# Shared-bank sums of recombined products and a second bank set for the down projections

## The chip, the cores and the metric

The kernel runs on one core of a Trainium2 chip. The metric is the device time of one execution in microseconds (us), the median of the runs. Names of engines: PE is TensorE (matmuls), PEld its weight loads, DVE is VectorE, ACT is ScalarE, POOL is GpSimd, SP the engine whose queue issues the DMAs. A bank is one 128 x 512 fp32 buffer of PSUM, where matmuls leave their sums.

## The reference

A backbone of two layers over 512 latent tokens and 256 context tokens, 1024 wide, in fp32. Each layer has a mixer and a feed-forward part with a convolution; the change is inside the latter alone.

```python
D_MODEL = 1024; SEQ = 512; CTX_LEN = 256; DEPTH = 2; D_FF = 2816; CONV_W = 3
...
def conv_ffn(h, w_up, conv_w, conv_b, w_down):
    t_len = h.shape[1]
    up = h @ w_up
    gate, val = up[..., :D_FF], up[..., D_FF:]
    pad = CONV_W // 2
    gp = jnp.pad(gate, ((0, 0), (pad, pad), (0, 0)))
    gate_c = conv_b
    for j in range(CONV_W):
        gate_c = gate_c + gp[:, j:j + t_len] * conv_w[j]
    return (jax.nn.silu(gate_c) * val) @ w_down
...
    for l in range(DEPTH):
        with_ctx = l < DEPTH - 1
...
        xl = xl + g2 * conv_ffn(modulate(xl, norm_ffn_w[l], sh2, sc2), ffn_w_up[l],
                                ffn_conv_w[l], ffn_conv_b[l], ffn_w_down[l])
        if with_ctx:
            xc = xc + cg2 * conv_ffn(modulate(xc, norm_ffn_w[l], csh2, csc2), ffn_w_up[l],
                                     ffn_conv_w[l], ffn_conv_b[l], ffn_w_down[l])
```

Layer 0 carries latent and context tokens (768 columns), layer 1 the latent tokens alone (512 columns).

## The kernel before

Activations are held transposed: 128 features on the partitions, tokens as columns. Every fp32 operand is kept as a high and a low part, and `mm3` (lines 501 to 503) makes one product of three matmuls: high x high, high x low, low x high. The weights come by DMA as raw fp32 and are split on the way: ACT casts the high part (L390, L490), and POOL or DVE subtracts it to get the low part (L392, L492).

The feed-forward part goes over 22 tiles of 128 features (D_FF = 2816). The first two tiles of each layer are computed plainly. Tiles 2 to 21 use seven half-sized products, j = 0 to 6, in place of eight: the tokens are halved into `nh` columns (384 in layer 0, 256 in layer 1), the input halves are combined once, the weight halves are summed per tile by DVE (`sum`, L381 to L383 and L387), and each product is 4 x 3 = 12 matmuls. `up_products` adds the products up to the gate (`gate`, two halves `g1`, `g2`) and the value (`u`, `w`). Before the change each product has a bank of its own in turn, and DVE does one copy (L1178) and seven adds (L1172) per tile.

What follows per tile is here called the tail: ACT's first convolution step (L1198), four DVE steps (L1200, L1202), Silu on ACT (L1204), the multiply by `u` on POOL (L1205) and by `w` on DVE (L1206), the cast to the high part on ACT (L1208) and the low part on POOL (L1209).

After a group of tiles comes its down projection (`out_pass`): 8 output blocks `m`, for each of which the matmuls over the group's tiles go into a bank per token segment, and DVE adds the gated result to the residual stream `xl`, `xc` (`residual`, L1016). In layer 0 the groups are 3, 3, 3, 3, 3, 3 and 4 tiles, and a group's down projection runs in one piece after the first tile of the next group. In layer 1 the groups are 2 and then 4 at a time, and two blocks of the down projection run after each tile, 24 matmuls of 512 columns.

There are eight banks, four with the tag `mm` and four with `aux`; a bank is handed out again when its last reader is done. `u` and `w` come from the pool `tp` under the tag `t2k`, 3 buffers, which some of the weight sums share. Each engine works through its own queue in order. A scheduler sets the order in the queues from the order of the code, dependences and priorities (`tc.high_priority`); `_Stream` decides when the next weights are loaded and split, by the units in `PROD_UNITS`; `PROD_ON_V` lists the products whose low part DVE makes, per layer; `PROD_OWN` those with a buffer outside the common pool.

Of the kernel before, what the change touches and what calls it, by code (L numbers as in the profile page):

```python
# [11 lines left out]
F32 = mybir.dt.float32  # L12
# [4 lines left out]
ALU = mybir.AluOpType  # L17
# [3 lines left out]
P = 128  # L21
# [13 lines left out]

FF_GROUPS = ((3, 3, 3, 3, 3, 3, 4), (2, 4, 4, 4, 4, 4))
FF_PLAIN = (2, 2)
PROD_ON_V = ((2,), (0, 1, 2, 3))
PROD_OWN = ((6,), (0, 4, 5, 6))
PROD_UNITS = ((0,), (1, 2, 3), (4,), (5,), (6,))  # L40
PROD_USE = (0, 1, 2, 3, 4, 5, 6)
PROD_FIRST = (0, 1, 2, 3, 4, 5, 6)

# [1 line left out]
def _ff_per(layer, g):  # L47

    return 8 // FF_GROUPS[layer][g]


def prod_order(layer, t):

    return PROD_FIRST if t == FF_PLAIN[layer] else PROD_USE


def _ff_order(layer):
# [234 lines left out]
class _Stream:  # L292
# [4 lines left out]
    def __init__(self, nc, w, raw_pool, hl_pool, order, offs, split, last_pool, sums):  # L297
        self.nc, self.w, self.order, self.offs = nc, w, order, offs
        self.raw_pool, self.hl_pool, self.split, self.last_pool, self.sums = raw_pool, hl_pool, split, last_pool, sums
        self.raw, self.hl = {}, {}  # L300
        self.n_dma = self.n_unit = self.pos = 0
        self.units, self.items = [], []
        i = 0
        while i < len(order):
            kind, t = order[i]
            if kind[:2] == "up" and FF_PLAIN[int(kind[2:])] <= t < NFF:
                for u in PROD_UNITS:
                    self.units.append((i, u))
                self.items += [(kind, t, j) for j in prod_order(int(kind[2:]), t)]
                i += 2  # L310
            else:
                self.units.append((i, None))
                self.items.append(order[i])
                i += 1
        self.live, self.own = {}, set()
        self.part = None
# [104 lines left out]
def backbone(ctx: ExitStack, tc, w, xt, ada, vec, cst, msk, rop, wst, bs, pew, out):  # L421
    nc = tc.nc
    V, S, G, T = nc.vector, nc.scalar, nc.gpsimd, nc.tensor
# [72 lines left out]
    ws = _Stream(nc, w, wraw, whl, chunk_order(), chunk_offsets(), split, lambda l, dt=F32R: last_pool[l](dt),  # L496
                 lambda l, n: sum_pool[l](n))

    def mm3(ps, a, b, first, last):

        T.matmul(ps, a[0], b[0], start=first, stop=False)  # L501
        T.matmul(ps, a[0], b[1], start=False, stop=False)  # L502
        T.matmul(ps, a[1], b[0], start=False, stop=last)  # L503


    bg = {"gla": deque(), "ada": deque(), "sum": deque()}
# [508 lines left out]
    def residual(xs, ps, gate):  # L1015
        V.scalar_tensor_tensor(xs, ps, gate, xs, op0=ALU.mult, op1=ALU.add)  # L1016

    def out_pass(key, nk, src, dst, gcol, each, chunks=None):

        per = 8 // nk  # L1020
        for m in range(KD):
            if chunks is not None and m // per not in chunks:
                continue
            if m % per == 0:
                wh, wl = ws.next((key, m // per))
            d = dst(m)
            ps = [bank("mm") for _ in d]
            for k in range(nk):
                o = (m % per * nk + k) * P
                a = (wh[:, o:o + P], wl[:, o:o + P])  # L1030
                for s in range(len(d)):
                    mm3(ps[s][:, 0:d[s].shape[-1]], a, src[s][k], k == 0, k == nk - 1)
                if k % 3 == 2:
                    tick()
            for s in range(len(d)):
                residual(d[s], ps[s][:, 0:d[s].shape[-1]], gcol(m, s))
            each(m)
# [14 lines left out]
    def ffn(layer, X, src, parts, late, down_last):  # L1052
# [106 lines left out]
        def up_products(t, gate):  # L1159

            ts = [[(tv(i, kk)[:, 0, :], tv(i, kk)[:, 1, :]) for kk in range(4)] for i in range(3)]
            rhs = [xq(0, n1), ts[1], xq(4, n2), ts[0], ts[2], xq(4, n1), xq(0, n2)]

            def product(j, ps):
                h, l = ws.next((f"up{layer}", t, j))
                for kk in range(4):
                    mm3(ps[:, 0:nh], (h[:, kk * P:(kk + 1) * P], l[:, kk * P:(kk + 1) * P]), rhs[j][kk],
                        kk == 0, kk == 3)
                return ps[:, 0:nh]

            def add(o, a, b):
                V.tensor_tensor(o, a, b, op=ALU.add)  # L1172

            b1, b2, b4, b3 = bank("mm"), bank("mm"), bank("aux"), bank("aux")
            u = tp.tile([P, nh], F32, tag="t2k", name="u")
            w_ = tp.tile([P, nh], F32, tag="t2k", name="w")
            g1, g2, u, w_ = gate[:, n1], gate[:, n2], u[:], w_[:]
            todo = [((0,), lambda p: V.tensor_copy(g1, p[0])), ((0, 1), lambda p: add(u, g1, p[1])),  # L1178
                    ((1, 3), lambda p: add(w_, u, p[3])), ((2, 3), lambda p: add(g2, w_, p[2])),
                    ((3, 4), lambda p: add(u, u, p[4])), ((3, 4), lambda p: add(w_, w_, p[4])),  # L1180
                    ((1, 5), lambda p: add(g1, g1, p[5])), ((3, 4, 6), lambda p: add(u, u, p[6]))]
            banks = (b1, b2, b4, b3, b1, b2, b3)
            done = {}
            for j in prod_order(layer, t):
                done[j] = product(j, banks[j])
                for need, f in [x for x in todo if all(k in done for k in x[0])]:
                    f(done)
                todo = [x for x in todo if not all(k in done for k in x[0])]
            return u, w_

        plain = FF_PLAIN[layer]
        for kind, i, *cs in seq:
            if kind == "up" and i >= plain:
                gate = t1tile()
                u, w_ = up_products(i, gate)
                t1 = t1tile()
                cw = lambda j: vcol("convw", (layer * 3 + j) * NFF + i)
                S.activation(t1[:, 0:nw], gate[:, 0:nw], AF.Identity, bias=vcol("convb", layer * NFF + i), scale=cw(1))  # L1198
                for c0, b, bc, n in merged:
                    V.scalar_tensor_tensor(t1[:, c0 + 1:c0 + n], gate[:, c0:c0 + n - 1], cw(0), t1[:, c0 + 1:c0 + n],  # L1200
                                           op0=ALU.mult, op1=ALU.add)
                    V.scalar_tensor_tensor(t1[:, c0:c0 + n - 1], gate[:, c0 + 1:c0 + n], cw(2), t1[:, c0:c0 + n - 1],  # L1202
                                           op0=ALU.mult, op1=ALU.add)
                S.activation(t1[:, 0:nw], t1[:, 0:nw], AF.Silu)  # L1204
                G.tensor_tensor(t1[:, n1], t1[:, n1], u, op=ALU.mult)  # L1205
                V.tensor_tensor(t1[:, n2], t1[:, n2], w_, op=ALU.mult)  # L1206
                a = acttile()
                S.copy(a[:, 0, 0:nw], t1[:, 0:nw])  # L1208
                G.tensor_tensor(a[:, 1, 0:nw], t1[:, 0:nw], a[:, 0, 0:nw].bitcast(F32), op=ALU.subtract)  # L1209
                acts[i] = a  # L1210
            elif kind == "up":
                psg, psv = up(i, i == 0)
                t1 = t1tile()
                cw = lambda j: vcol("convw", (layer * 3 + j) * NFF + i)
                for c0, b, bc, n in merged:
                    S.activation(t1[:, c0:c0 + n], psg[b][:, 0:n], AF.Identity, bias=vcol("convb", layer * NFF + i),
                                 scale=cw(1))
                    V.scalar_tensor_tensor(t1[:, c0 + 1:c0 + n], psg[b][:, 0:n - 1], cw(0), t1[:, c0 + 1:c0 + n],
                                           op0=ALU.mult, op1=ALU.add)
                    V.scalar_tensor_tensor(t1[:, c0:c0 + n - 1], psg[b][:, 1:n], cw(2), t1[:, c0:c0 + n - 1],  # L1220
                                           op0=ALU.mult, op1=ALU.add)
                S.activation(t1[:, 0:nw], t1[:, 0:nw], AF.Silu)
                for c0, b, bc, n in merged:
                    V.tensor_tensor(t1[:, c0:c0 + n], psv[b][:, 0:n], t1[:, c0:c0 + n], op=ALU.mult)
                a = acttile()
                S.copy(a[:, 0, 0:nw], t1[:, 0:nw])
                G.tensor_tensor(a[:, 1, 0:nw], t1[:, 0:nw], a[:, 0, 0:nw].bitcast(F32), op=ALU.subtract)
                acts[i] = a
                if i == plain - 1:
                    drain("sum")  # L1230
                    replace()
            else:
                n = groups[i]
                tl = [acts[starts[i] + j] for j in range(n)]
                pairs = [[(a[:, 0, c0:c0 + w_], a[:, 1, c0:c0 + w_]) for a in tl] for c0, b, bc, w_ in merged]
                if i == len(groups) - 1:
                    down_last(f"down{layer}_{i}", n, pairs)
                else:
                    out_pass(f"down{layer}_{i}", n, pairs, xdst, lambda m, s: mods[layer][:, 40 + m, s:s + 1],
                             lambda m: None, cs[0])  # L1240


    xl, xc = load_x()
# [189 lines left out]
    A = []  # L1433
# [389 lines left out]
```

## Time and profile before

| what | value |
|---|---|
| median of 3 runs | 1714.34 us (1713.84 to 1714.83) |
| the profiled execution | 1713.79 us, its span 1712.0 us |
| PE busy | 94% of the span, 11206 matmuls |
| DVE, ACT, POOL busy | 68%, 40%, 43% |
| layer 0's feed-forward stretch 540 to 965 us | PE busy 412.66 of 425.00 us |
| layer 1's feed-forward stretch 1450 to 1660 us | PE busy 194.04 of 210.00 us |

In a profile line, times are us unless marked ns. A timeline line reads: start, duration, engine, source line, operation, output<-inputs, shape, and in brackets the idle time of that engine before it and what ended it. A line of groups reads: line, engine, operation, names, shapes, count | busy, mean ns of one | idle time before, and what ended most of it. A line of stretches reads: from:to, length, then PE, PEld, DVE, ACT and POOL busy (instructions), PE's granted clock, DMA share and GB/s. Line numbers are those of the kernel that ran; the changed kernel's are 6 lower up to `out_pass`, and up to 7 higher behind `up_products`.

### The profile page before, as it was taken

How to read it: one execution, taken by the hardware profiler on the slowest of the kernel's cores; microseconds unless marked ns; L12 is line 12 of the kernel's file. 1: busy time of each engine (PE TensorE's matmuls, PEld its weight loads, DVE VectorE, ACT ScalarE, POOL GpSimd, SP SyncE). 2: the span in 40 equal slices, each digit the busy share in tenths (PEclk: the TensorE clock that was granted, in tenths of full speed). 3: DMA queues.
4: the chain of work that ended last, by engine and by line, in shares of the span. 5: the costliest groups of instructions: out<-in, count | busy, mean ns of one | idle time of the engine just before them, and what ended most of it. 6: DMA issues, size and time to landing. Idle time of an engine off the chain costs nothing.

```text
span 1712.0 us, 28429 instructions
## 1 busy us (share of the span) xinstructions
PE 1616.2 (94%) x11206; PEld 1430.8 (84%) x11206; DVE 1164.5 (68%) x2124; ACT 685.9 (40%) x1374; POOL 735.6 (43%) x456
## 2 busy tenths in 40 slices
PE   7999999989999999999999999988899989999999
PEld 6777777778899989889898888566799978888887
DVE  6347676752756756666665784777866898888884
ACT  4323333523453323233232453556554544343431
POOL 1221223344535556566564423411127356555551
PEclk9999999999999999999999999999999999999999
DMA  8453334323412122121221223632015222222222
GB/s 341 136 196 113 136 112 148 114 96 110 124 35 78 53 67 79 58 78 37 76 82 54 88 87 105 243 118 100 24 50 174 86 74 88 90 96 88 98 79 82
DMA packets 53206, 175.11 MB, mean 102 GB/s; under 512 B 5713, under 2 KB 7761, under 8 KB 53073
## 3 DMA queue, kind: packets, MB, share of 16 engines
q1 hardware_dynamic: 51632, 170.66, 30.4%
q10 hardware_dynamic: 1440, 2.64, 0.4%
q8 instruction: 88, 1.44, 0.3%
q14 instruction: 46, 0.37, 0.1%
HBM read 171.18 MB, written 2.10 MB: 101 GB/s over the span
## 4 chain that ended last, share of the span: by engine, by line
PE 62%; DVE 22%; issue 5%; POOL 4%; ACT 4%; DMA 3%; DVEq 0%; ACTq 0%; SPq 0%; POOLq 0%
PE mm L501 14%; PE mm L502 14%; PE mm L503 14%; PE aux L501 3%; PE aux L502 3%; PE aux L503 3%; DVE wp L392 3%; DMA raw<-in_w_dram 2%; PE aux L570 2%; POOL wl L492 2%; DVE qk L858 1%; DVE kt L382 1%; DVE qk L856 1%; DVE kt L383 1%; ACT wp L390 1%
## 5 line engine op out<-in xcount | busy, mean ns | idle before, releaser
L492 POOL TENSOR_TENSOR wl<-raw,wh 128x1024 fp32r<-128x1024 f32 (+6 forms) x143 | 311.3, 2179 | 508.2 <-ACT wh L490 471.0
L490 ACT CAST wh<-raw 128x1024 fp32r<-128x1024 f32 (+5 forms) x155 | 146.5, 945 | 138.2 <-PE mm L502 71.6
L392 POOL TENSOR_TENSOR wp<-sum,wp 128x512 fp32r<-128x512 f32 x80 | 111.7, 1403 | 155.8 <-ACT wp L390 155.8
L501 PE MATMUL mm<-slot,wh 128*128 128x512 f32 (+1 forms) x480 | 163.5, 341 | 13.3 <-DVE xl L1016 10.7
L502 PE MATMUL mm<-slot,wh 128*128 128x512 f32 (+1 forms) x480 | 162.3, 338 | 1.0 <-POOL slot L1209 0.7
L503 PE MATMUL mm<-slot,wl 128*128 128x512 f32 (+1 forms) x480 | 161.5, 337 | 0.0
L1016 DVE SCALAR_TENSOR_TENSOR xl<-mm,mods,xl 128x512 f32<-128x512 f32 (+1 forms) x128 | 90.8, 712 | 96.0 <-PE mm L503 95.9
L392 POOL TENSOR_TENSOR wp<-raw,wp 128x512 fp32r<-128x512 f32 x80 | 113.7, 1428 | 69.2 <-ACT wp L390 69.2
L501 PE MATMUL mm<-xt,wh 128*128 128x256 f32 (+1 forms) x384 | 135.6, 355 | 0.0
L390 ACT CAST wp<-sum 128x512 fp32r<-128x512 f32 x100 | 60.8, 620 | 186.1 <-DVE sum L387 80.3
L503 PE MATMUL mm<-xt,wl 128*128 128x512 f32 (+1 forms) x384 | 130.2, 340 | 0.0
L502 PE MATMUL mm<-xt,wh 128*128 128x512 f32 (+1 forms) x384 | 130.2, 340 | 0.0
L501 PEld LDWEIGHTS mm<-slot,wh 128*128 128x128 f32 x480 | 90.5, 189 | 27.1 <-DVE xl L1016 11.9
L501 PE MATMUL mm<-lt,wh 128*128 128x512 f32 (+2 forms) x308 | 106.9, 347 | 0.0
L503 PE MATMUL mm<-lt,wl 128*128 128x512 f32 (+2 forms) x308 | 106.4, 346 | 0.0
L502 PE MATMUL mm<-lt,wh 128*128 128x512 f32 (+2 forms) x308 | 106.3, 345 | 0.0
L390 ACT CAST wp<-raw 128x512 fp32r<-128x512 f32 x100 | 61.8, 618 | 96.3 <-PE mm L502 36.6
L502 PEld LDWEIGHTS mm<-slot,wh 128*128 128x128 f32 x480 | 90.6, 189 | 11.7 <-POOL slot L1209 1.1
L503 PEld LDWEIGHTS mm<-slot,wl 128*128 128x128 f32 x480 | 90.7, 189 | 10.4
L501 PEld LDWEIGHTS mm<-xt,wh 128*128 128x128 f32 x384 | 72.9, 190 | 25.9 <-issue 16.8
L1205 POOL TENSOR_TENSOR t<-t,u 128x384 f32<-128x384 f32 (+1 forms) x40 | 46.0, 1151 | 99.3 <-ACT t L1204 96.1
L501 PE MATMUL aux<-kt,wp 128*128 128x256 f32 x240 | 69.8, 291 | 19.7 <-DVE w L1172 19.7
(363 smaller groups left out, 4962.5 us busy)
## 6 DMA issues: line engine op xcount, KB each, us to landing
raw<-in_w_dram SPq DMA_DIRECT2D x162, 512.0 KB, 3.6
ada_t<-in_ada_dram SPq DMA_DIRECT2D x80, 512.0 KB, 4.5
raw<-in_w_dram SPq DMA_DIRECT2D x31, 384.0 KB, 3.1
wp<-in_w_dram SPq DMA_DIRECT2D x20, 512.0 KB, 4.6
kt<-in_ada_dram SPq DMA_DIRECT2D x16, 512.0 KB, 6.1
raw<-in_w_dram SPq DMA_DIRECT2D x10, 256.0 KB, 2.6
xl<-in_xt_dram SPq DMA_DIRECT2D x2, 1024.0 KB, 9.4
out_dram<-xl SPq DMA_DIRECT2D x8, 256.0 KB, 2.0
```

The costliest lines, as they stand in the source:

```text
L382: V.tensor_tensor(s2, s1, a11, op=ALU.subtract)
L383: V.tensor_tensor(s4, a12, s2, op=ALU.subtract)
L390: S.copy(h, a)
L392: e.tensor_tensor(l, a, h.bitcast(F32), op=ALU.subtract)
L490: S.copy(h, raw)
L492: e.tensor_tensor(l, raw, h.bitcast(F32), op=ALU.subtract)
L501: T.matmul(ps, a[0], b[0], start=first, stop=False)
L502: T.matmul(ps, a[0], b[1], start=False, stop=False)
L503: T.matmul(ps, a[1], b[0], start=False, stop=last)
L570: T.matmul(ps[32 * q:32 * q + 32, :], sc_pad[:, k, :], t[:, j * 512:(j + 1) * 512], start=(k == 0), stop=(k == KD - 1))
L1016: V.scalar_tensor_tensor(xs, ps, gate, xs, op0=ALU.mult, op1=ALU.add)
L1205: G.tensor_tensor(t1[:, n1], t1[:, n1], u, op=ALU.mult)
```

## The change

Products that enter the same sums are now accumulated by PE in one bank, without a new start: 0, 1 and 3 in bank A, 4 and 6 in C, 5 in B, 2 in E. Between them ACT copies the sum so far out of the bank (`u` after 0 and again after 1, `w` after 4, `g2` after 3), and DVE makes four adds. The order of the products is 0, 4, 5, 1, 6, 2, 3, in the weights' units too. All eight are issued with a higher priority. In layer 1, `u` and `w` lie in columns of the tiles `gate` and `t1` that were not used; in layer 0 they stay in `t2k`. In layer 1 the low part of product 0's weights moves from DVE to POOL. The down projections, all but each layer's last, take their banks alternately from `mm` and `aux`.

```diff
-PROD_ON_V = ((2,), (0, 1, 2, 3))
+PROD_ON_V = ((2,), (1, 2, 3))
 PROD_OWN = ((6,), (0, 4, 5, 6))
-PROD_UNITS = ((0,), (1, 2, 3), (4,), (5,), (6,))
-PROD_USE = (0, 1, 2, 3, 4, 5, 6)
-PROD_FIRST = (0, 1, 2, 3, 4, 5, 6)
+PROD_UNITS = ((0,), (4,), (5,), (1, 2, 3), (6,))
+PROD_USE = (0, 4, 5, 1, 6, 2, 3)
...
-    def out_pass(key, nk, src, dst, gcol, each, chunks=None):
+    def out_pass(key, nk, src, dst, gcol, each, chunks=None, tags=("mm", "mm")):
...
-            ps = [bank("mm") for _ in d]
+            ps = [bank(tags[m % 2]) for _ in d]
...
-            def product(j, ps):
+            def product(j, ps, first=True, last=True):
                 h, l = ws.next((f"up{layer}", t, j))
                 for kk in range(4):
                     mm3(ps[:, 0:nh], (h[:, kk * P:(kk + 1) * P], l[:, kk * P:(kk + 1) * P]), rhs[j][kk],
-                        kk == 0, kk == 3)
-                return ps[:, 0:nh]
...
+                        first and kk == 0, last and kk == 3, skip_group_check=True)
...
+            A, C, B, E = bank("mm"), bank("mm"), bank("aux"), bank("aux")
+            pa, pb, pc, pe = A[:, 0:nh], B[:, 0:nh], C[:, 0:nh], E[:, 0:nh]
+            if layer:
+                t1 = t1tile()
+                u, w_ = gate[:, nw:nw + nh], t1[:, nw:nw + nh]
+            else:
+                t1 = None
+                u = tp.tile([P, nh], F32, tag="t2k", name="u")[:]
+                w_ = tp.tile([P, nh], F32, tag="t2k", name="w")[:]
+            g1, g2 = gate[:, n1], gate[:, n2]
+
+            def soon(f, *args, **kw):
+                with tc.high_priority(200):
+                    f(*args, **kw)
+
+            product(0, A, last=False)
+            soon(S.copy, u, pa)
+            product(4, C, last=False)
+            soon(S.copy, w_, pc)
+            product(5, B)
+            soon(V.tensor_tensor, g1, u, pb, op=ALU.add)
+            product(1, A, False, False)
+            soon(S.copy, u, pa)
+            product(6, C, False)
+            soon(V.tensor_tensor, u, u, pc, op=ALU.add)
+            product(2, E)
+            product(3, A, False)
+            soon(V.tensor_tensor, w_, w_, pa, op=ALU.add)
+            soon(S.copy, g2, pa)
+            soon(V.tensor_tensor, g2, g2, pe, op=ALU.add)
+            return u, w_, t1
...
-                             lambda m: None, cs[0])
+                             lambda m: None, cs[0], ("mm", "aux"))
```

How the queues change is seen at three places. In their rows, numbers behind names tell the buffers' generations apart, and the brackets hold the engines and DMA queues that the instruction waits for (Pool is POOL, Activation is ACT).

First, ACT in layer 0, where one product tile follows directly on another. Before, from the tail of the one tile (`t1_6730`):

```order
L1198 ACTIVATE t1_6730<-t1_6592,vt_73 128x768 [waits DVE_49]
L390 CAST wp_6749<-raw_6484 128x512 [waits DMAHW3_49,PE_49]
L390 CAST wp_6767<-raw_6626 128x512 [waits DMAHW4_49,PE_49,Pool_49]
L1204 ACTIVATE t1_6730<-t1_6730 128x768 [waits DVE_49,Activation_49]
L1208 CAST slot_6739<-t1_6730 128x768 [waits DVE_49,Pool_49]
L390 CAST wp_6811<-sum_6814 128x512 [waits DVE_49,PE_49]
L390 CAST wp_6812<-sum_6815 128x512 [waits DVE_49,PE_49]
```

Now, from the last copy of the one tile (`t1_6585` is its gate, `t1_6715` its tail), with the copies of the next (`u_6732`, `w_6733`) in between:

```order
L1179 COPY t1_6585<-mm_6586 128x384 [waits DVE_49]
L1205 ACTIVATE t1_6715<-t1_6585,vt_73 128x768 [waits DVE_49]
L1179 COPY u_6732<-mm_6728 128x384 [waits PE_49,Pool_49]
L384 CAST wp_6749<-raw_6484 128x512 [waits DMAHW3_49]
L384 CAST wp_6767<-raw_6626 128x512 [waits DMAHW4_49]
L1211 ACTIVATE t1_6715<-t1_6715 128x768 [waits DVE_49,Activation_49]
L1179 COPY w_6733<-mm_6729 128x384 [waits PE_49,Pool_49]
L1215 CAST slot_6724<-t1_6715 128x768 [waits DVE_49]
```

The copy into `w_6733` stands behind the Silu of the tile before and waits for POOL. POOL's rows at this place now are these, where the multiply with `u_6590`, the `u` of the tile before, is the last reader of that buffer:

```order
L386 TENSOR_TENSOR wp_6749<-raw_6484,wp_6749 128x512 [waits DMAHW3_49,Activation_49]
L386 TENSOR_TENSOR wp_6767<-raw_6626,wp_6767 128x512 [waits PE_49,DMAHW4_49,Activation_49,Pool_49]
L1212 TENSOR_TENSOR t1_6715<-t1_6715,u_6590 128x384 [waits Activation_49]
L1216 TENSOR_TENSOR slot_6724<-t1_6715,slot_6724 128x768 [waits Activation_49,Pool_49]
L386 TENSOR_TENSOR wp_6785<-sum_6786,wp_6785 128x512 [waits PE_49,Activation_49]
```

Second, POOL in layer 1 for one tile of the steady part. Before (`t_15505` is the tail, `lt` the tile's split result):

```order
L1205 TENSOR_TENSOR t_15505<-t_15505,u 128x256
L1209 TENSOR_TENSOR lt<-t_15505,lt 128x512
L392 TENSOR_TENSOR wp<-wp 128x512
L492 TENSOR_TENSOR wl<-raw,wh 128x1024
L392 TENSOR_TENSOR wp<-sum,wp 128x512
L392 TENSOR_TENSOR wp<-raw,wp 128x512
```

Now:

```order
L486 TENSOR_TENSOR wl<-raw,wh 128x1024
L1212 TENSOR_TENSOR t_15525<-t_15525,t_15520 128x256
L1216 TENSOR_TENSOR lt<-t_15525,lt 128x512
L386 TENSOR_TENSOR wp<-raw,wp 128x512
L386 TENSOR_TENSOR wp<-sum,wp 128x512
L386 TENSOR_TENSOR wp<-raw,wp 128x512
L386 TENSOR_TENSOR wp<-wp 128x512
```

The split `wl` of the down projection's weights stands ahead of the multiply, and the row for product 0 is new. On ACT the same tile now has, with the cast of the result and the copies of the next tile's first and second product:

```order
L1211 ACTIVATE t_15525<-t_15525 128x512
L384 CAST wp<-kt 128x512
L1215 CAST lt<-t_15525 128x512
L1179 COPY t_15692<-mm 128x256
L384 CAST wp<-raw 128x512
L384 CAST wp<-sum 128x512
L1179 COPY t_15697<-mm 128x256
```

The copy of the first product stands behind the cast to `lt`, which waits for POOL's multiply.

Third, DVE in a down projection of layer 0. Before, all residual adds read `mm`:

```order
L1016 SCALAR_TENSOR_TENSOR xl_3774<-mm_5778,mods0_81,xl_3774 128x512 [waits PE_49]
L1016 SCALAR_TENSOR_TENSOR xc_3775<-mm_5779,mods0_81,xc_3775 128x256 [waits PE_49]
L1016 SCALAR_TENSOR_TENSOR xl_3774<-mm_5800,mods0_81,xl_3774 128x512 [waits PE_49]
L1016 SCALAR_TENSOR_TENSOR xc_3775<-mm_5801,mods0_81,xc_3775 128x256 [waits PE_49]
L1016 SCALAR_TENSOR_TENSOR xl_3774<-mm_5822,mods0_81,xl_3774 128x512 [waits PE_49]
```

Now:

```order
L1010 SCALAR_TENSOR_TENSOR xl_3774<-mm_5862,mods0_81,xl_3774 128x512 [waits PE_49]
L1010 SCALAR_TENSOR_TENSOR xc_3775<-mm_5863,mods0_81,xc_3775 128x256 [waits PE_49]
L1010 SCALAR_TENSOR_TENSOR xl_3774<-aux_5884,mods0_81,xl_3774 128x512 [waits PE_49]
L1010 SCALAR_TENSOR_TENSOR xc_3775<-aux_5885,mods0_81,xc_3775 128x256 [waits PE_49]
L1010 SCALAR_TENSOR_TENSOR xl_3774<-mm_5909,mods0_81,xl_3774 128x512 [waits PE_49]
```

Every second block reads `aux`; the count and order of the adds is the same.

More of the change, by code (lines that the diff above doesn't have):

```diff
@@ L37 @@
 FF_PLAIN = (2, 2)
-PROD_ON_V = ((2,), (0, 1, 2, 3))
+PROD_ON_V = ((2,), (1, 2, 3))
 PROD_OWN = ((6,), (0, 4, 5, 6))
-PROD_UNITS = ((0,), (1, 2, 3), (4,), (5,), (6,))
-PROD_USE = (0, 1, 2, 3, 4, 5, 6)
-PROD_FIRST = (0, 1, 2, 3, 4, 5, 6)
+PROD_UNITS = ((0,), (4,), (5,), (1, 2, 3), (6,))
+PROD_USE = (0, 4, 5, 1, 6, 2, 3)
 def _ff_per(layer, g):
     return 8 // FF_GROUPS[layer][g]
-def prod_order(layer, t):
-    return PROD_FIRST if t == FF_PLAIN[layer] else PROD_USE
 def _ff_order(layer):
@@ L308, in __init__ @@
                     self.units.append((i, u))
-                self.items += [(kind, t, j) for j in prod_order(int(kind[2:]), t)]
+                self.items += [(kind, t, j) for j in PROD_USE]
                 i += 2
@@ L497, in backbone, with mm3 @@
                  lambda l, n: sum_pool[l](n))
[L499 to L503, printed above, removed]
+    def mm3(ps, a, b, first, last, **kw):
+        T.matmul(ps, a[0], b[0], start=first, stop=False, **kw)
+        T.matmul(ps, a[0], b[1], start=False, stop=False, **kw)
+        T.matmul(ps, a[1], b[0], start=False, stop=last, **kw)
     bg = {"gla": deque(), "ada": deque(), "sum": deque()}
@@ L1167, in product @@
                     mm3(ps[:, 0:nh], (h[:, kk * P:(kk + 1) * P], l[:, kk * P:(kk + 1) * P]), rhs[j][kk],
-                        kk == 0, kk == 3)
-                return ps[:, 0:nh]
[L1171 to L1188, printed above, removed]
@@ L1189, in up_products @@
-            return u, w_
+                        first and kk == 0, last and kk == 3, skip_group_check=True)
[8 more added lines that the diff above has]
+                w_ = tp.tile([P, nh], F32, tag="t2k", name="w")[:]
@@ L1194, in ffn @@
                 gate = t1tile()
-                u, w_ = up_products(i, gate)
-                t1 = t1tile()
+                u, w_, t1 = up_products(i, gate)
+                t1 = t1 or t1tile()
                 cw = lambda j: vcol("convw", (layer * 3 + j) * NFF + i)
```

## Prediction

> **What bounds the kernel now.** I read the page's engine totals first, then the table of stretches for the two feed-forward halves that the change touches, then TensorE's groups in them with what ended their idle time, and last the timeline around one wait of each kind.
>
> ```profile
> span 1712.0 us, 28429 instructions
> PE 1616.2 (94%) x11206; PEld 1430.8 (84%) x11206; DVE 1164.5 (68%) x2124; ACT 685.9 (40%) x1374; POOL 735.6 (43%) x456
> ...
> 540.00:965.00 425.00, 412.66 (x2343) 391.08 (x2342) 279.30 (x415) 140.23 (x203) 249.80 (x165) 1.00 0.22 66
> 1360.00:1450.00 90.00, 82.21 (x568) 76.56 (x567) 78.25 (x117) 36.75 (x59) 47.08 (x33) 0.96 0.28 94
> 1450.00:1660.00 210.00, 194.04 (x1325) 177.81 (x1323) 177.64 (x256) 85.85 (x137) 121.01 (x75) 1.00 0.26 88
> ...
> L501 PE MATMUL mm<-slot,wh 128*128 128x512 f32 x141 | 56.5, 401 | 11.4 <-DVE xl L1016 10.7 <-ACT t L1204 0.7
> L501 PE MATMUL aux<-kt,wp 128*128 128x256 f32 x152 | 43.7, 288 | 13.0 <-DVE w L1172 13.0
> L501 PE MATMUL mm<-lt,wp 128*128 128x256 f32 x48 | 14.4, 300 | 3.0 <-DVE t L1178 3.0
> ```
>
> TensorE (PE) is the bound, so only what it waits for counts. In layer 0 (the stretch from 540, with six of the down projections) it is idle 425.00 − 412.66 = 12.3 us; 11.4 of them lie before the down projections' matmuls, which wait for a residual add on VectorE (DVE), and the products wait for nothing. In layer 1 (from 1450) it is idle 16.0 us, all in the products: 13.0 for the third bank (`w` is added late) and 3.0 for the first product's copy. The granted clock is 1.00 in both, so the clock is left out. One wait of each kind:
>
> ```profile
> 617.17 1.89 POOL L1209 TENSOR_TENSOR slot<-t,slot 128x768 fp32r<-128x768 f32 x1 [0.95 <-ACT slot L1208]
> 617.29 2.32 DVE L383 TENSOR_TENSOR sum<-raw,sum 128x512 f32<-128x512 f32 x1
> 619.54 0.74 DVE L1016 SCALAR_TENSOR_TENSOR xl<-mm,mods,xl 128x512 f32<-128x512 f32 x1
> 620.33 0.50 PE L501 MATMUL mm<-slot,wh 128*128 128x512 f32 x1 [1.80 <-DVE xl L1016]
> 620.67 0.39 PE L502 MATMUL mm<-slot,wh 128*128 128x512 f32 x1
> 620.89 0.40 PE L503 MATMUL mm<-slot,wl 128*128 128x512 f32 x1
> 635.06 0.68 DVE L383 TENSOR_TENSOR sum<-raw,sum 128x512 f32<-128x512 f32 x1
> ...
> 1453.70 0.36 PE L501 MATMUL mm<-lt,wp 128*128 128x256 f32 x1 [0.26 <-DVE t L1178]
> 1457.83 0.36 PE L501 MATMUL aux<-kt,wp 128*128 128x256 f32 x1 [1.08 <-DVE w L1172]
> 1458.02 0.28 PE L502 MATMUL aux<-kt,wp 128*128 128x256 f32 x1
> 1458.14 0.28 PE L503 MATMUL aux<-kt,wp 128*128 128x256 f32 x1
> ```
>
> In layer 0 a sum of weights that takes 0.68 us by itself took 2.32 while a GpSimd (POOL) subtract ran from 617.17 to 619.06; the residual add queued behind it came late and PE stood 1.80 us. So a DVE instruction with two SBUF inputs and a POOL instruction shut each other out. The Trainium skill says the same on its page "SBUF — State Buffer", section "Who interferes with whom": whichever issues first holds the shared ports for its whole instruction and the other blocks, and the two L383 rows agree with that. Its rule is not needed for the sum; if the two only slowed each other the next tail below would lose its long end.
>
> A wait costs more than its idle time: the last matmul's record (0.28) outlasts the pitch (1458.14 − 1458.02 = 0.12) by 0.16, and by 0.17 for 512 columns (0.39 against 0.22). So one layer 1 tile loses 1.08 + 0.26 + 2 × 0.16 = 1.66 us, and a layer 0 group 11.4/6 = 1.9 plus two or three times 0.17, 2.3 us.
>
> **The change, part by part.**
>
> *Two bank sets in the down projections.* Consecutive output blocks alternate between four banks, so a residual has one block more before its banks are wanted: 9 matmuls of 512 columns at 0.22 and 9 of 256 at 0.12, 3.1 us. The lateness to cover is the 1.8 us above. I take all of the six groups' wait as gone: 6 × 2.3 = −14 us; the ends are −14 and −10 (some waits remain where two blocked sums follow each other). These banks are those of the products too, but a product starts behind the down's last residuals only, as before.
>
> *Eight DVE operations become four DVE adds and four ScalarE (ACT) copies*, 20 tiles in each layer. PE's matmuls are the same in number. DVE has 68% and ACT 40% of the span, neither bounds, so the prices matter only in the chains below. Those chains need ACT's price for a copy out of a bank, which I take from its casts of the same size, and the tail of a layer 0 tile, twice:
>
> ```profile
> L1132 ACT CAST slot<-aux 128x384 fp32r<-128x384 f32 x12 | 5.7, 481 | 8.5 <-PE aux L1131 8.5
> L1132 ACT CAST kt<-aux 128x256 fp32r<-128x256 f32 x12 | 4.3, 376 | 1.2 <-PE aux L1131 1.2
> ...
> 644.93 0.34 PE L503 MATMUL mm<-slot,wp 128*128 128x384 f32 x1
> ...
> 646.32 0.34 PE L502 MATMUL mm<-slot,wp 128*128 128x384 f32 x1
> ...
> 648.97 0.55 DVE L1172 TENSOR_TENSOR t<-t,mm 128x384 f32<-128x384 f32 x1 [1.09 <-PE mm L503]
> 649.56 1.03 ACT L1198 ACTIVATE t<-t,vt 128x768 f32<-128x768 f32 x1
> 649.72 1.30 POOL L392 TENSOR_TENSOR wp<-raw,wp 128x512 fp32r<-128x512 f32 x1 [0.87 <-ACT wp L390]
> 650.62 0.95 DVE L1200 SCALAR_TENSOR_TENSOR t<-t,vt,t 128x511 f32<-128x511 f32 x1 [1.10 <-ACT t L1198]
> 651.96 1.66 DVE L1202 SCALAR_TENSOR_TENSOR t<-t,vt,t 128x511 f32<-128x511 f32 x1
> 654.05 1.43 DVE L1202 SCALAR_TENSOR_TENSOR t<-t,vt,t 128x255 f32<-128x255 f32 x1
> 656.50 1.40 POOL L1205 TENSOR_TENSOR t<-t,u 128x384 f32<-128x384 f32 x1 [1.30 <-ACT t L1204]
> ...
> 665.42 1.03 ACT L1198 ACTIVATE t<-t,vt 128x768 f32<-128x768 f32 x1 [0.72 <-DVE t L1172]
> 671.39 1.32 POOL L1205 TENSOR_TENSOR t<-t,u 128x384 f32<-128x384 f32 x1 [2.54 <-ACT t L1204]
> ...
> 681.14 0.74 DVE L1202 SCALAR_TENSOR_TENSOR t<-t,vt,t 128x511 f32<-128x511 f32 x1
> 682.31 0.48 DVE L1202 SCALAR_TENSOR_TENSOR t<-t,vt,t 128x255 f32<-128x255 f32 x1
> ```
>
> *A new wait in layer 0.* The copy that empties bank C (the second product's, into `w`) is now an ACT write into a buffer of the three that `u`, `w` and a weight sum share, and the order shows it waiting for POOL: for the multiply of the tile before, which is the last reader of that tile's `u`. The fifth product adds into C and waits for the copy. Before, `w` was first written by a DVE add after the fourth product, and its bank was none that the next product wanted at once. What the fifth product has in hand is four products, 48 matmuls at (646.32 − 644.93)/8 = 0.174, 8.35 us, if no down projection lies between the two tiles. That holds for 13 tiles of layer 0 (one in the first group, two in each of the six others); where a down projection lies between, its matmuls cover the wait and I cost it at nothing.
>
> The chain against these 8.35 us: the last product's end 0.16, `w`'s add 0.55, ACT's copy into the gate 0.48, the final add 0.55, three hand-overs of 0.05 together 0.15: 1.9. The order makes the copy wait for the add, though both only read the bank; side by side they would save 0.5, 6 us over 13 tiles. (The Trainium skill's page "PSUM — Partial Sum Buffer", section "PSUM bank collisions raise a hardware error", says that two engines, readers included, must not be on one bank at a time; no run here shows that.) Then the tail from the first convolution step to the end of POOL's multiply: 656.50 + 1.40 − 649.56 = 8.3 in the first, 671.39 + 1.32 − 665.42 = 7.3 in the second. `u`'s add (0.55, like the row at 648.97) no longer stands inside it, where it did before; two weight sums of 0.68 now stand ahead of the tail's DVE part, covered by the convolution step's 1.03 but for 0.3. That leaves 8.1 or 7.1. Then the copy 0.48 and PE's restart about 0.15: 10.6 or 9.6, so a stall of 2.3 or 1.3 us. The long tail holds POOL locks: 1.66 for 0.74, 1.43 for 0.48, 0.95 for about 0.8, together 2.0; without any the stall is 0.3, with one more lock of 0.9 it is 3.2. I take 2.3, the long row, because the rows that the change leaves on POOL beside the tail (four or five weight splits of 1.30) are those that lengthened it. 13 × 2.3 = +30 us; ends 13 × 0.3 = +4 and 13 × 3.2 = +42.
>
> *Layer 1.* Both bank waits of before lose their cause: the copies go to ACT with two products between copy and next sum, and `u` and `w` lie in unused columns, free early. What is late next is read from the other engines' groups of the stretch from 1450:
>
> ```profile
> L492 POOL TENSOR_TENSOR wl<-raw,wh 128x1024 fp32r<-128x1024 f32 x13 | 37.0, 2844 | 0.0
> L1205 POOL TENSOR_TENSOR t<-t,u 128x256 f32<-128x256 f32 x12 | 11.8, 980 | 37.6 <-ACT t L1204 37.6
> L392 POOL TENSOR_TENSOR wp<-raw,wp 128x512 fp32r<-128x512 f32 x12 | 21.0, 1752 | 0.0
> L1198 ACT ACTIVATE t<-t,vt 128x512 f32<-128x512 f32 x12 | 9.8, 817 | 21.2 <-DVE t L1172 21.2
> L1208 ACT CAST lt<-t 128x512 fp32r<-128x512 f32 x12 | 7.4, 620 | 13.1 <-POOL t L1205 13.1
> L1202 DVE SCALAR_TENSOR_TENSOR t<-t,vt,t 128x511 f32<-128x511 f32 x12 | 9.0, 752 | 0.4
> ```
>
> Up to 13 × 1.66 = 21.6 us (13 tiles, the count of the L492 row) can go. But POOL's queue now has the 2.84 us split of the down weights ahead of the multiply, where the multiply came first; and ACT's copy of the first product stands behind the cast that waits for this multiply. The fourth product wants that copy. It is due 24 matmuls of the down projection (0.22 each, 5.3) and three products (36 × 0.12 = 4.3) after the tile before, 9.6 us. The chain: first part 1.5 (as above at about 0.4 a step), convolution 0.82 + 2 × 0.75, Silu about 0.7 (a little under the convolution step of the same width), so 4.5; then 2.84 + 0.98 if the split starts just before, 8.3; one lock of about 0.9 in the convolution, 9.2; cast 0.62 and copy 0.38, 10.2: a stall of 0.6. Without the split in front it is none; with a convolution step locked behind the split (up to 2.84 − 0.75 = 2.1) it is over 2. I take 0.6, the order's own case: 13 × (1.66 − 0.6) = −13.8, ends −21.6 and +5.
>
> The 0.75 and 0.98 rows also price the product that moves from DVE's splits to POOL's: 20 × 1.75 = 35 us of POOL, of which 12 tiles (21) in a stretch where it has 210 − 121 = 89 free. It costs nothing It costs nothing but the queueing above..
>
> The early tiles (1360 to 1450) have 90 − 82.2 = 7.8 us idle. They have no steady down projection before each, so both waits can appear there: between −7.8 and +10 I take +3. The last tile's multiply and subtract come later on POOL: +1. Layer 1 together: −13.8 + 3 + 1 = −10.
>
> **Sum.** −14 + 30 − 10 = +6 us on the profiled execution's 1713.79 (span 1712.0 and 1.8 around it), which is 0.55 under the median of 1714.34: 1720 to 1721. I give 1721.
>
> **Rivals.**
> *The copy of `w` comes in time (or nearly).* If the tail meets few locks (the clean rows 0.74 and 0.48 speak for it, the other two tails against), the stall is 0.3 to 1.0: +4 to +13, and the sum −20 to −11, 1694 to 1703, say 1699. It decides for faster when the stall is under 1.5 us.
> *The stall is between,* 1.3 to 1.9 as in the second tail: 17 to 25, sum −7 to +1 and about 1713. No difference to tell.
> *Layer 1 gains nothing:* DVE's convolution step is caught behind the 2.84 us split in most tiles, its 1.66 comes back as 1.7 or more: −14 + 30 + 4 = +20, 1734. Against it: the split starts when ACT has cast its weights, which need not meet the convolution.
> *The down projections keep their wait* because the residual is late by more than a block: then −14 is near −3, sum +17, 1731. The 1.80 us row against 3.1 us in hand speaks against it.
>
> **Chances.** The forecast 0.50 (its own range 1717 to 1728), in time 0.22, between 0.17, no gain in layer 1 0.08, down waits kept 0.03. Faster by over 0.2% (3.4 us, about what a measurement of this kernel can tell from no change): 0.24, from the first rival and part of the second. Within: 0.16. Slower: 0.60. The range leaves the best half of the first rival out and takes in the third: 1702 to 1735.
>
> **What would show it.** In layer 0's stretch, TensorE's idle before down matmuls goes from 11.4 to below 3; a new idle stands before the fifth product's first matmul, put down to ACT's copy of `w`, in two of three tiles of a group and about 2 us each; POOL's multiply ends that copy's wait. In layer 1 the 13.0 before the third bank is gone and a smaller one, about 7, stands before the fourth product. Wrong would be: no idle at the fifth product (then the tail is shorter than the rows say), or a longer down projection.

## The result, and the profile after

The changed kernel takes 1733.96 us (median of 4 runs, 1731.56 to 1737.17) against 1714.09 us before; the ratio is 1.0119, with a 95% interval of 1.010 to 1.0138. It is 20 us slower where 7 were forecast: 1733.96 lies inside the stated range, the direction is right, and the size is three times too small. The profiled execution took 1737.17 us, 3.2 above its median; the one of before took 1713.79.

The totals of the page after, and the same three stretches as before (from:to, length, PE, PEld, DVE, ACT, POOL busy, granted clock, DMA share, GB/s):

```profile
span 1735.4 us, 28297 instructions
PE 1625.3 (94%) x11206; PEld 1438.6 (83%) x11206; DVE 1123.5 (65%) x1944; ACT 737.1 (42%) x1534; POOL 763.1 (44%) x476
...
540.00:965.00 425.00, 400.96 (x2249) 379.92 (x2247) 248.75 (x334) 155.50 (x256) 238.36 (x158) 0.98 0.20 64
1360.00:1450.00 90.00, 80.29 (x560) 73.97 (x559) 72.72 (x96) 48.31 (x97) 55.45 (x35) 0.98 0.26 88
1450.00:1660.00 210.00, 199.23 (x1360) 183.08 (x1359) 173.03 (x205) 101.08 (x189) 137.37 (x89) 1.00 0.27 93
```

In layer 0, PE's idle time has doubled, 425.00 − 400.96 = 24.0 us for 12.3, and the granted clock, 1.00 before, is 0.98. In layer 1's steady part the idle fell only from 16.0 to 10.8 us. PE's groups in the first and the third of these stretches tell which waits they are:

```profile
L495 PE MATMUL mm<-xt,wp 128*128 128x384 f32 x132 | 47.8, 362 | 23.3 <-ACT w L1179 23.3
L495 PE MATMUL mm<-slot,wh 128*128 128x512 f32 x70 | 27.4, 392 | 0.0
...
L495 PE MATMUL mm<-kt,wp 128*128 128x256 f32 x201 | 57.7, 287 | 10.8 <-ACT t L1179 10.8
```

The down projections' 11.4 us are gone to 0.0. In their place 23.3 us stand before the fifth product, put down to ACT's copy into `w`, the line that the prediction named. In layer 1 the 13.0 and 3.0 are gone, and 10.8 stand before the fourth product. One new wait of layer 0, in the timeline:

```profile
655.64 2.17 DVE L1207 SCALAR_TENSOR_TENSOR t<-t,vt,t 128x511 f32<-128x511 f32 x2
655.91 3.07 POOL L386 TENSOR_TENSOR wp<-raw,wp 128x512 fp32r<-128x512 f32 x2 [1.63 <-ACT wp L384]
657.74 2.18 DVE L1209 SCALAR_TENSOR_TENSOR t<-t,vt,t 128x511 f32<-128x511 f32 x2
660.02 0.85 ACT L1211 ACTIVATE t<-t 128x768 f32<-128x768 f32 x1 [3.67 <-DVE t L1209]
660.94 1.36 POOL L1212 TENSOR_TENSOR t<-t,u 128x384 f32<-128x384 f32 x1 [1.96 <-ACT t L1211]
662.34 0.48 ACT L1179 COPY w<-mm 128x384 f32<-128x384 f32 x1 [1.48 <-POOL t L1212]
662.87 0.44 PE L495 MATMUL mm<-xt,wp 128*128 128x384 f32 x1 [2.32 <-ACT w L1179]
663.78 0.52 PE L496 MATMUL mm<-xt,wp 128*128 128x384 f32 x1
664.10 0.52 PE L497 MATMUL mm<-xt,wp 128*128 128x384 f32 x1
```

It reads upwards: PE waits for the copy, the copy for POOL's multiply, this for the Silu, and that for convolution steps which POOL's splits held up (two rows of two steps take 2.2 us each). The last two rows show something that no term of the sum had: after the wait the matmuls follow each other at 0.32 us (663.78 to 664.10), not at 0.174. The granted clock in the 3.3 us behind this wait and behind the next one, equally long (2.34):

```profile
662.90:666.20 3.30, 3.30 (x12) 3.30 (x13) 0.00 (x0) 2.59 (x5) 2.51 (x2) 0.59 0.02 5
681.70:685.00 3.30, 3.30 (x19) 3.30 (x20) 0.55 (x1) 1.75 (x3) 2.52 (x2) 1.00 0.00 0
```

Twelve matmuls in place of nineteen: PE ran at half clock for some 3.4 us after the first and not after the second. Eleven matmuls at 0.32 in place of 0.174 cost 1.6 us. Of the twelve waits of 2.26 to 2.35 us in layer 0, seven were followed by such a stretch. PE counts as busy in it, so it is in no idle time.

The trace's own record of the granted clock tells which waits these are. The stretches start whole multiples of 3.413 us apart (in layer 0 at 530.41, 663.53, 738.62, 813.71, 834.19, 892.22 and 967.31), so time is cut into fixed windows of that length, and what counts is how much of a wait falls into one window. The seven waits had 1.86 to 2.32 us of their idle time in the window just before the stretch; the other five straddled a boundary, with 1.89 us at most in one window.

### The profile page after: what moved, and what is told of

Its sections match the earlier page's. It is cut to its first block, busy times and chain, and to the rows that moved or that the text cites. A ratio compares the mean times of both kernels' runs of the same rounds, so it can differ in the third digit from the quotient of the medians.

```text
span 1735.4 us, 28297 instructions
## 1 busy us (share of the span) xinstructions
PE 1625.3 (94%) x11206; PEld 1438.6 (83%) x11206; DVE 1123.5 (65%) x1944; ACT 737.1 (42%) x1534; POOL 763.1 (44%) x476
## 4 chain that ended last, share of the span: by engine, by line
PE 55%; DVE 24%; ACT 6%; issue 5%; POOL 5%; DMA 3%; SPq 0%; POOLq 0%; ACTq 0%; DVEq 0%
PE mm L495 12%; PE mm L497 12%; PE mm L496 12%; DVE t L1209 3%; PE aux L495 3%; PE aux L496 3%; PE aux L497 3%; DVE wp L386 3%; PE aux L564 2%; POOL wp L386 2%; POOL t L1212 2%; DVE t L1207 2%; POOL wl L486 2%; DMA wp<-in_w_dram 2%; DVE qk L852 1%
## 5 line engine op out<-in xcount | busy, mean ns | idle before, releaser
L386 POOL TENSOR_TENSOR wp<-raw,wp 128x512 fp32r<-128x512 f32 x100 | 144.8, 1451 | 72.7 <-ACT wp L384 72.7
L496 PE MATMUL mm<-slot,wh 128*128 128x512 f32 (+1 forms) x336 | 113.6, 338 | 1.2 <-POOL slot L1216 0.9
L495 PE MATMUL mm<-slot,wh 128*128 128x512 f32 (+1 forms) x336 | 113.3, 338 | 0.9 <-ACT slot L1215 0.9
L495 PE MATMUL mm<-kt,wp 128*128 128x256 f32 x320 | 93.0, 291 | 22.2 <-ACT t L1179 22.2
L497 PE MATMUL mm<-slot,wl 128*128 128x512 f32 (+1 forms) x336 | 113.3, 338 | 0.0
L1010 DVE SCALAR_TENSOR_TENSOR xl<-mm,mods,xl 128x512 f32<-128x512 f32 (+1 forms) x84 | 58.3, 694 | 77.5 <-PE mm L497 77.3
L496 PE MATMUL mm<-kt,wp 128*128 128x256 f32 x320 | 90.5, 283 | 0.0
L497 PE MATMUL mm<-kt,wp 128*128 128x256 f32 x320 | 90.4, 282 | 0.0
L495 PE MATMUL mm<-xt,wp 128*128 128x384 f32 x160 | 58.7, 367 | 28.7 <-ACT w L1179 28.7
L386 DVE TENSOR_TENSOR wp<-kt,wp 128x512 fp32r<-128x512 f32 x60 | 76.0, 1272 | 14.5 <-ACT wp L384 10.1
L495 PEld LDWEIGHTS mm<-kt,wp 128*128 128x128 f32 x320 | 61.3, 192 | 27.7 <-ACT t L1179 26.8
L497 PE MATMUL mm<-slot,wp 128*128 128x384 f32 x240 | 80.8, 337 | 0.0
L496 PE MATMUL mm<-slot,wp 128*128 128x384 f32 x240 | 80.4, 335 | 0.0
```

What stands on the lines that cost most here:

```text
L386: e.tensor_tensor(l, a, h.bitcast(F32), op=ALU.subtract)
L495: T.matmul(ps, a[0], b[0], start=first, stop=False, **kw)
L496: T.matmul(ps, a[0], b[1], start=False, stop=False, **kw)
L497: T.matmul(ps, a[1], b[0], start=False, stop=last, **kw)
```

## The experiments

The theory after this reading: layer 0's copy into `w` costs some 31 us of waits and 10 us of half clock, the second bank set gains 15, and layer 1 is about even. The first four runs take these apart; the median of before beside them was 1714.54 us. A change of a few us is read from the traces too, since the medians of before in the three sets differ by up to 1.6.

**The second bank set alone.** On the kernel before:

```diff
-            ps = [bank("mm") for _ in d]
+            ps = [bank(tags[m % 2]) for _ in d]
...
-                             lambda m: None, cs[0])
+                             lambda m: None, cs[0], ("mm", "aux"))
```

> The kernel before with one part of the change alone: the down projections take their banks alternately from the two sets. If that removes the wait for the residual adds (11.4 us of idle and the restarts, about 15 us in the trace before), 1714 becomes 1697 to 1702, and the idle before the down matmuls in layer 0 is under 2 us. Rival: the late residuals push the next products' banks, or DVE, instead, and the gain comes back as a wait in the products: 1708 or more.

Measured: 1698.35 us, ratio 0.9909 (0.9873 to 0.9944). In layer 0's stretch PE is busy without a gap:

```profile
540.00:950.00 410.00, 410.00 (x2356) 392.57 (x2355) 281.81 (x420) 139.85 (x202) 249.39 (x165) 1.00 0.24 70
```

So this part of the change gains 16 us by itself, and nothing is late in its place.

**Layer 1 summed as before, layer 0 as changed.** `PROD_UNITS`, `PROD_USE` and `PROD_ON_V` hold the values of before for layer 1, and `up_products` runs its old body there:

```diff
+            if layer == 1:
+                b1, b2, b4, b3 = bank("mm"), bank("mm"), bank("aux"), bank("aux")
+                ...
+                return u, w_, None
```

> The changed kernel, but layer 1's products are summed as before (seven banked products, eight DVE operations, product 0's split on DVE); layer 0 and the banks of the down projections as changed. Theory: all of the loss is layer 0's wait for the copy into w, and layer 1 came out even, so 1734 stays within 3 us (1731 to 1737). If layer 1 gained the 10 us that were forecast and the loss of layer 0 is larger, this is 1744; if layer 1 lost as well, 1724 or less.

Measured: 1736.62 us (1734.95 to 1738.96). With the new sums in layer 1 it was 1733.96: the runs of the two overlap, so by the medians layer 1 came out even or a little better (2.7 us). Layer 0's products are left with 1736.62 − 1698.35 = 38 us of loss.

**Two buffers for `w` in layer 0.** On the changed kernel:

```diff
-                w_ = tp.tile([P, nh], F32, tag="t2k", name="w")[:]
+                w_ = l0c.tile([P, nh], F32, tag="w2k", name="w", bufs=2)[:]
```

> The changed kernel, but layer 0's w has two buffers of its own and no longer waits for POOL's multiply of the tile before. Theory: the wait before the fifth product goes (12 x 2.5 us and one of 1.0 in the trace after, 31 us) and with it the stretches at half clock behind it (seven, about 1.5 us each, 10 us): 1734 - 41 = 1693, between 1689 and 1698. Rival 1: the chain behind it, from the last product over the convolution to the copies, is late for its own reasons, and the fifth product goes on waiting for ACT: 1710 or more. Rival 2: half clock comes from something else than these waits: 1703.

Measured: 1694.55 us, ratio 0.9881 (0.9855 to 0.9907): 39 us less than the changed kernel, by one line. Layer 0's stretch:

```profile
540.00:955.00 415.00, 414.98 (x2377) 396.25 (x2375) 270.76 (x350) 170.03 (x278) 256.84 (x166) 1.00 0.23 70
```

No idle time, and a granted clock of 1.00. The wait that the prediction named, with what it drags behind it, is the whole loss of layer 0. Both rivals fall.

**One buffer for `w`** (the same line with `bufs=1`), to shorten the wait and not remove it:

> The changed kernel, but layer 0's w has one buffer of its own: its copy waits for DVE's multiply with the w of the tile before, which ends about 0.8 us before POOL's multiply with u (660.90 + 0.56 against 660.94 + 1.36 in the trace after). So 12 waits of 2.3 become about 1.5: 10 us less by the waits themselves, 1724. If half clock follows on waits over some 1.8 us alone (seven of twelve at 2.3, two of six at 1.8 and none of fourteen at 1.6 or less in the two traces), its 10 us go too: 1714. Rival: half clock stays at about as many waits as now: 1723 to 1726.

Measured: 1729.13 us (1728.77 to 1730.04). Neither number was met, because only the second wait of each group became shorter. The two waits of a group, from the timeline, and the granted clock in the 3.3 us behind each:

```profile
583.85 1.05 POOL L1212 TENSOR_TENSOR t<-t,u 128x384 f32<-128x384 f32 x1 [1.96 <-ACT t L1211]
583.97 1.35 DVE L1213 TENSOR_TENSOR t<-t,w 128x384 f32<-128x384 f32 x1
...
585.88 0.47 PE L495 MATMUL mm<-xt,wp 128*128 128x384 f32 x1 [2.41 <-ACT w L1179]
603.73 0.44 PE L495 MATMUL mm<-xt,wp 128*128 128x384 f32 x1 [1.41 <-ACT w L1179]
```

```profile
585.90:589.20 3.30, 3.30 (x11) 3.30 (x12) 0.00 (x0) 1.56 (x3) 3.30 (x3) 0.54 0.19 28
603.70:607.00 3.30, 3.27 (x19) 3.27 (x20) 0.56 (x1) 1.21 (x2) 2.36 (x3) 1.00 0.02 7
```

Before the first, POOL's multiply started 0.12 us ahead of DVE's and held it to 1.35 us instead of 0.55: the order of two instructions decides 0.8 of the 1.0 us between the two waits. For the clock the run is a clear case within one kernel: of the six waits of 2.41 us five were followed by half clock (2.09 us or more in one window; the sixth straddled a boundary, with 1.73), of the six of 1.41 none.

**Layer 1.** The next four runs stand on the kernel with two buffers (1694.55); before was 1712.99 us beside them. In the trace of the changed kernel, two tiles in turn:

```profile
1458.67 2.40 POOL L486 TENSOR_TENSOR wl<-raw,wh 128x1024 fp32r<-128x1024 f32 x1 [3.60 <-ACT t L1205]
1458.84 2.78 DVE L1209 SCALAR_TENSOR_TENSOR t<-t,vt,t 128x511 f32<-128x511 f32 x1
1462.42 0.96 POOL L1212 TENSOR_TENSOR t<-t,t 128x256 f32<-128x256 f32 x1 [1.35 <-ACT t L1211]
1463.42 0.62 ACT L1215 CAST lt<-t 128x512 fp32r<-128x512 f32 x1 [0.56 <-POOL t L1212]
1463.95 0.36 ACT L1179 COPY t<-mm 128x256 f32<-128x256 f32 x1
1464.36 0.38 PE L495 MATMUL mm<-kt,wp 128*128 128x256 f32 x1 [1.42 <-ACT t L1179]
...
1475.54 0.75 DVE L1209 SCALAR_TENSOR_TENSOR t<-t,vt,t 128x511 f32<-128x511 f32 x1
1475.86 2.69 POOL L486 TENSOR_TENSOR wl<-raw,wh 128x1024 fp32r<-128x1024 f32 x1 [4.10 <-issue]
1478.52 0.91 POOL L1212 TENSOR_TENSOR t<-t,t 128x256 f32<-128x256 f32 x1
1480.41 0.39 PE L495 MATMUL mm<-kt,wp 128*128 128x256 f32 x1 [0.27 <-ACT t L1179]
```

In the first, the split began 0.17 us ahead of DVE's convolution step, which then took 2.78 us; in the second it began 0.32 us behind it, and only the multiply queued. PE lost 1.42 and 0.27 of idle time. Of the fifteen such steps that meet a split in this trace, seven were caught (2.77 to 2.98 us) and eight not (0.74 to 0.75). The edits, each alone: the down projection's split in layer 1 on DVE,

```diff
-        e = G if kind in on_pool else V
+        e = G if kind in on_pool and kind[:5] != "down1" else V
```

> The kernel with two buffers for w (1694.6), and in layer 1 the low part of the down projection's weights is subtracted by DVE, not POOL. In the trace after, POOL's 2.4 to 2.8 us for this split stand ahead of the multiply in every tile and in every second tile block a DVE convolution step for 2 us as well, and the fourth product waits 0.4 and 1.6 us in turn. Theory (the split on POOL is what layer 1's new wait hangs on): most of the 20 us of waits at that product go, 1694 - 12 = 1682. Rival: DVE is loaded by 13 splits of about 1.2 us or more and is late itself, or the multiply and the cast alone make the copy late: 1692 or more.

product 0's split back on DVE,

```diff
-PROD_ON_V = ((2,), (1, 2, 3))
+PROD_ON_V = ((2,), (0, 1, 2, 3))
```

> The kernel with two buffers for w, and in layer 1 the low part of product 0's weights back on DVE as before the change. It takes 20 x 1.3 to 1.75 us out of POOL's row and puts 20 x 0.84 us on DVE. If POOL's row as a whole is late (the split for the down projection begins late because product 0's stands before it), part of the wait at the fourth product goes: 1686. If POOL has room, as the prediction had it, nothing changes: 1694.

the multiply on DVE, and this together with the edit before it:

```diff
-                G.tensor_tensor(t1[:, n1], t1[:, n1], u, op=ALU.mult)
+                (V if layer else G).tensor_tensor(t1[:, n1], t1[:, n1], u, op=ALU.mult)
```

> The kernel with two buffers for w, and in layer 1 the multiply with u on DVE, not POOL, so that it no longer queues behind the down projection's split. If the wait at the fourth product hangs on this queueing alone (2.4 to 2.8 us of split, then 0.98), it loses most of it: 1684. If it hangs on the lock between the split and DVE's instructions of two SBUF inputs, the multiply on DVE is blocked by the split all the same: 1692 to 1695.

> Both of the last two together, with two buffers for w. If each works on its own cause, their gains add; if POOL's row is what matters, product 0's split alone gives 8 and the multiply some 4 more: 1682.

Measured: the down projection's split on DVE 1677.00 us, product 0's split on DVE 1682.25, the multiply on DVE 1689.14, the last two together 1680.48. The next rows show the second convolution step on DVE (12 of it in the stretch from 1405 to 1600), in the kernel with two buffers and then with each of the first three edits in turn. The second block also has DVE's price for the split that moved:

```profile
L1209 DVE SCALAR_TENSOR_TENSOR t<-t,vt,t 128x511 f32<-128x511 f32 x12 | 24.5, 2039 | 0.4
```

```profile
L486 DVE TENSOR_TENSOR wl<-raw,wh 128x1024 fp32r<-128x1024 f32 x12 | 14.6, 1219 | 0.0
L1209 DVE SCALAR_TENSOR_TENSOR t<-t,vt,t 128x511 f32<-128x511 f32 x12 | 9.0, 751 | 0.4
```

```profile
L1209 DVE SCALAR_TENSOR_TENSOR t<-t,vt,t 128x511 f32<-128x511 f32 x12 | 11.1, 927 | 0.4
```

```profile
L1209 DVE SCALAR_TENSOR_TENSOR t<-t,vt,t 128x511 f32<-128x511 f32 x12 | 32.6, 2718 | 0.4
```

Moving the split gains 17.6 us, more than the 12 expected: the step is back at 0.75 us, the split no longer stands ahead of POOL's multiply, and what took POOL 2.4 to 2.8 us takes DVE 1.2. Product 0's split, costed at nothing in the prediction, is worth 12 us. Without it on POOL the big split begins about 0.35 us behind the step in the steady part, and only the first of the twelve steps is still caught:

```profile
1461.13 0.75 DVE L1209 SCALAR_TENSOR_TENSOR t<-t,vt,t 128x511 f32<-128x511 f32 x1
1461.48 2.66 POOL L486 TENSOR_TENSOR wl<-raw,wh 128x1024 fp32r<-128x1024 f32 x1 [5.78 <-issue]
```

The multiply on DVE gains 5 by its shorter queue, although the lock now hits nearly every tile (2.72); the expectation's two readings were each half right. The two gains don't add (14.1 us together, not 12.3 + 5.4 = 17.7). With the big split alone on DVE, PE is busy for 193.74 of 195.00 us of the steady part:

```profile
1405.00:1600.00 195.00, 193.74 (x1335) 179.64 (x1334) 161.67 (x211) 99.67 (x186) 106.53 (x76) 1.00 0.30 101
```

**What the shared-bank sums bring.** Three last runs, beside 1714.34 us for before: the kernel of before with the second bank set and the split on DVE; the changed one with layer 0's products summed as before and the split on DVE; and two buffers with both splits on DVE.

> The kernel before with two of the edits and no shared banks: the down projections' two bank sets (1698.4), and layer 1's split for the down projection on DVE. It tells whether the shared-bank sums have a part in the 1677 us. Theory: layer 1 before waited for DVE itself (w's add and the first copy), which has eight operations per tile there; 13 more splits on it bring nothing or a loss, 1696 to 1704. Rival: the split on POOL was the trouble by itself, with the old sums too, and 1682 or less comes without the new ones.

> Layer 0's products as before the change, layer 1's in shared banks with the down projection's split on DVE, the two bank sets in the down projections. Theory: once w has its own buffers, the shared-bank sums bring nothing in layer 0, since nothing was waited for in its products before: the same as 1677, within 3 us. If they bring something there, 1681 or more.

> Two buffers for w, and in layer 1 both the down projection's split and product 0's on DVE. What waits are left in layer 1 (8.6 and 2.6 us, nearly all before the steady part) can fall a little: 1675, not under 1672; or DVE gets too full and it is 1680 or more.

Measured: 1697.31, 1679.79 and 1674.33 us, in this order. With the old sums the split on DVE gains nothing (1698.35 without it). In layer 1's steady part of that run, from 1430 to 1640, PE waits 16.7 us for the first product's DVE copy,

```profile
L501 PE MATMUL aux<-kt,wp 128*128 128x256 f32 x144 | 41.6, 289 | 1.8 <-DVE w L1172 1.1
...
L501 PE MATMUL mm<-lt,wp 128*128 128x256 f32 x48 | 14.4, 300 | 16.7 <-DVE t L1178 16.7
```

so in layer 1 the change of the sums is worth 17.5 us (1697.31 to 1679.79, with layer 0 summed as before in both) once the big split is off POOL. The change there is a bundle: the new sums with four DVE operations fewer, the order of the products, the higher priority, the places of `u` and `w`, and product 0's split. The last run has that split on DVE again and is no slower, so the split isn't what gains; no run separates the others. That room on DVE is what counts fits the 16.7 us above, but isn't shown alone. In layer 0 the new sums bring nothing that can be told: 1679.79 against 1677.00 is within these runs' spread (1676.85 to 1682.19). The last run beats both kernels: 1674.33 us, ratio 0.9774 (0.9758 to 0.9789) to the kernel before. Its lead of 2.7 us over the run with one split on DVE isn't certain, since the two intervals overlap.

## Why the prediction was right and wrong

*The down projections' two bank sets: right.* −14 was forecast; alone they gave −16.

*The new wait in layer 0: right in place, cause and length.* 2.3 us at each of 13 tiles were forecast; the trace has twelve waits of 2.26 to 2.35 us of idle time, 2.4 to 2.5 with the 0.16 by which a record outlasts the pitch, and one of 0.84; together some 31 us for the 30 forecast. The long tail was the row to take: from ACT's first convolution step (653.92) to the end of POOL's multiply (662.30) it took 8.4 us for the 8.1 of the sum. The four DVE steps took 4.5 us in sum, as in the tail at 649.56, though the longer ones were not the same steps.

*The clock: the step that failed first.* "The granted clock is 1.00 in both, so the clock is left out" was read from a kernel whose waits there are shorter, and the cost of the new waits was counted as idle time only. Seven stretches of half clock at 1.6 us in this execution, five in that of the kernel with layer 1 as before, are 8 to 11 us that had no term, and the loss was 38 us for the 30 forecast. With the windows of 3.413 us and a limit of about 1.87 us, a wait of 2.3 us at a random place is caught in (3.41 − 2.32 + 2 × 0.45)/3.41, nearly 0.6 of the cases; that is an estimate from the figures above, 0.9 us per wait, and the 13 forecast waits make 12 us. The trace of before had a hint: of its six waits of 1.56 to 1.84 us in the down projections, one (at 763) was followed by such a stretch.

*Layer 1: the second failure, −2.7 for −10.* The forecast took the split ahead of the multiply and one lock of 0.9 as the case of every tile, a stall of 0.6. The runs show two cases, mostly in turn: 0.27 us of idle time, and 1.42 where the step is caught behind the split. With the 0.16 of the restart, which the 1.66 counted and the 0.6 did not, the two average 1.0 us. The catching was the third rival's mechanism, at a chance of 0.08, and that the split's start "need not meet the convolution" was no price. That this rival's 1734 is the time measured is luck: its layer 1 loses 4 us and its layer 0 loses 30, where the runs show a gain of about 3 and a loss of 38. Nothing in the rows of before told which of the two comes first, so it should have been taken as open in each tile, and its 2.1 us as half likely.

Counted by the same matmul's start in both traces, the product tiles ahead of the steady part lose about 2.6 us (forecast 3), the steady ones gain 6.5 (14), and the end loses 1.6 (1): together a gain of 2.3. Another 3.8 us are lost before the first product, at the norm ahead of layer 1's feed-forward part, where this execution ran 6.8 us at half clock and that of before none; the kernel with layer 1 as before ran as long at half clock there, so the new sums aren't its cause. Moving product 0's split was costed at "nothing but the queueing above"; undone, it gives 12 us.

In sum: −16 + 38 − 3 = +19, against 20 measured, where the prediction had −14 + 30 − 10 = +6. The bank sets came out 2 better than forecast, the clock 8 worse and layer 1 7 worse.

The Trainium skill's rule on the shared ports (page "SBUF — State Buffer", section "Who interferes with whom") is borne out where the starts lie apart: 2.78 us for a 0.75 us step when POOL started 0.17 us earlier, 0.75 when it started 0.3 us or more later. In near ties the order of the records doesn't tell who waits: in five of the seven caught steps POOL's record starts 0.03 to 0.04 us behind DVE's, and in one step that was not caught 0.05 us behind.

## What to carry to other kernels

When a copy out of a bank moves into a buffer from a small rotating pool, ask who reads that buffer last, and on which engine's queue; here one line that gave `w` two buffers turned 20 us of loss into 20 us of gain. A wait on TensorE of some 2 us can cost more than its length: price it with the half clock behind it, here 1.6 us in about half of the cases (12 of 24 in two traces), or cut it to 1.4 us, where none followed. Where a long POOL instruction and DVE instructions with two SBUF inputs can start within some tenths of a microsecond of each other, price the collision as about as likely as not (7 of 15 steps here), and try moving the long one: here it was even shorter on DVE (1.2 for 2.4 to 2.8 us).

## What the runs showed of the hardware

After waits of 2.26 to 2.42 us before a product, TensorE ran at half clock (0.32 us for 0.174 per 384 columns) for about 3.4 us in 7 of 12 cases in the changed kernel and 5 of 6 with one buffer; two waits of the same length in one kernel can differ in it. After waits of 1.4 us there was none. Within each of the thirteen traces the half-clock stretches start whole multiples of 3.413 us apart, and in layer 0's feed-forward part a wait was followed by one when some 1.83 to 1.89 us or more of it lay in one such window: of two waits of before that lay whole in one, that of 1.83 us (at 763) was, that of 1.80 (at 620) was not. The Trainium skill's page "TensorE: Matmul & The Clock Gate", Part 1, says that activity is watched in free-running windows of about 3.4 us; the length of these stretches and their starts agree with that. Its table in "Why this matters for your kernels" asks for no gaps over about 3 us; here 2.3 us were already enough in about half of the cases.
